# Local attention of a hybrid encoder layer: the strided queries copied side by side by GpSimd ahead of the score products

## The chip, the cores and the metric

The kernel runs on one core of a Trainium2 chip. The metric is the device time of one execution in microseconds (us), as the median over several runs. The core has a matrix engine (TensorE; PE in the profile, with its weight loads shown apart as PEld), VectorE (DVE), ScalarE (ACT), GpSimd (POOL) and SyncE (SP), which here issues most of the DMAs. Each engine works through its own queue in order.

## The reference

One layer on 2048 tokens of width 1024: an input projection feeds two attention parts side by side, whose outputs are normed, projected and added to the residual; a convolutional feed-forward part follows. The change touches part A, local attention over 8 heads of 64 dimensions, which is computed three times with windows of different dilation and mixed by the softmax denominators:

```python
SWA_PATTERNS = ((128, 1), (512, 4), (2048, 16))      # window, dilation

def dilated_band_attention(q, k, v, dilation, n_side):
    ...
    qr = to_residue(q).reshape(B * dilation, nblk, blk, H, Dh).astype(jnp.float32)
    ...
    s = jnp.einsum('znqhd,znkhd->znhqk', qr, kb) * (Dh ** -0.5)
    s = jnp.where(valid[None, :, None, :, :], s, NEG_INF)
```

`to_residue` puts tokens that are `dilation` apart next to each other, so a block of 128 queries of the second pattern is every 4th token, and one of the third every 16th. Part B is a dense attention (multi-head latent attention, "MLA" below) with 4 heads over all 2048 keys.

## The kernel before, in words

**Arithmetic.** Every float32 product is made of products of operands that are split into a rounded part (hi) and the rest (lo). In the local attention the stationary operand of a score product is a block of 128 queries (`qhh`, then `qll`), the moving operand are the keys `kst`.

**Local attention** is `swa` (L519). For a head, `prep` (L540) loads queries and keys in 8 pieces (`raw`, L547, two buffers), transposes them on TensorE and stores `qhh`, `qll` and `kst`, head dimension on partitions and the 2048 tokens along the free axis. Then come 12 groups, four each of pattern 3 (dilation 16), 2 (dilation 4) and 1 (dilation 1), in this order. A group has 4 blocks of 128 queries, and `scores` (L589) issues for each block two matmuls at L601, one with `qhh` and one with `qll` as weights. `operands` (L577) picks the slices:

```python
                return [q[:, P * b:P * b + P] for q in qs], ks[:, 192 + P * b:448 + P * b], side
...
                return [q[:, o:o + 509:4] for q in qs], ks[:, o:o + 1021:4], side
...
            return [q[:, r::16] for q in qs], ks[:, 256 + r:256 + S:16], "all"
```

Pattern 1 reads weights and keys side by side, pattern 2 every 4th column of both, pattern 3 every 16th of both. A block moves 256 keys in patterns 1 and 2 and 128 in pattern 3. VectorE then takes each block out of PSUM with its mask and its maximum (L604). While head h is scored, head h-1 goes on through `numerators` (exponentials), `flip` (transposes, L622), `load_v` and `values` (L635 for pattern 3, L641 for 1 and 2).

**MLA** is `mla_prologue` (L252, which loads and splits its weights, then per 512 tokens transposes `ct`, L286, and writes queries, keys and values to DRAM) and `_mla_core` (L351): score products at L417, transposes at L441, value products at L67 to L69. GpSimd splits the queries `q` of each pair of blocks (L61, L62, L401, L402) and, at a new head, its keys `knh`, `knl` and values `vh`, `vl` (L61, L62).

**Order.** `attention` (L775) is a loop that takes steps of the two parts in a fixed proportion; a scheduler with a model of the engines' times then sets the order in which each engine's queue gets the instructions. Tiles come from pools with a number of buffers (`bufs`); a tile waits until the readers of the one that had its buffer are done. After local attention has ended, the rest of MLA runs with the output projection (`phase_out`) beside it, and the feed-forward part follows.

Of the kernel before, what the change touches and what calls it, by code (L numbers as in the profile page):

```python
# [11 lines left out]
F32 = mybir.dt.float32  # L12
F32R = mybir.dt.float32r
# [7 lines left out]
P = 128  # L21
# [230 lines left out]
def mla_prologue(tc, g, ps_t, ps_s):  # L252


    nc = tc.nc
    with ExitStack() as ctx:
        def pool(name, bufs, **kw):
            return ctx.enter_context(tc.tile_pool(name="mp_" + name, bufs=bufs, reuse_waits="tile", **kw))

        wp = pool("w", 1)  # L260
        op = pool("o", 2)
        raw = wp.tile([P, 2, 768], F32, name="uq_raw")
        nc.sync.dma_start(raw, g.w_uq[0].rearrange("(k p) c -> p k c", p=P))
        uq = (wp.tile([P, 2, 768], F32R, name="uq_hi"), wp.tile([P, 2, 768], F32R, name="uq_lo"))
        nc.scalar.copy(uq[0], raw)
        nc.vector.tensor_tensor(uq[1], raw, uq[0].bitcast(F32), ALU.subtract)
        raw2 = wp.tile([P, 1024], F32, name="ukv_raw")
        nc.sync.dma_start(raw2, g.w_ukv[0])
        ukv = (wp.tile([P, 1024], F32R, name="ukv_hi"), wp.tile([P, 1024], F32R, name="ukv_lo"))
        nc.scalar.copy(ukv[0], raw2)  # L270
        nc.vector.tensor_tensor(ukv[1], raw2, ukv[0].bitcast(F32), ALU.subtract)
        gq = wp.tile([P, 3], F32, name="gq")
        nc.sync.dma_start(gq[:, 0:2], g.q_norm_g[0].rearrange("(k p) -> p k", p=P))
        nc.sync.dma_start(gq[:, 2:3], g.kv_norm_g[0].rearrange("(k p) -> p k", p=P))

        for G in range(4):
            cs = slice(512 * G, 512 * G + 512)
            ct = [op.tile([P, 2, 512], F32, name="ct", bufs=3) for _ in range(2)]
            for i in range(2):
                nc.sync.dma_start(ct[i], g.cd[4 * G + 2 * i:4 * G + 2 * i + 2].rearrange("T p c -> p T c"))  # L280
            cq = [op.tile([P, 2, 512], F32R, name=f"cq{i}", bufs=1) for i in range(2)]
            ckv = [op.tile([P, 512], F32R, name=f"ckv{i}", bufs=1) for i in range(2)]
            for k in (2, 3, 0, 1):
                ps = ps_t.tile([P, 512], F32, name="pst")
                for t in range(4):
                    nc.tensor.transpose(ps[:, P * t:P * t + P], ct[t // 2][:, t % 2, P * k:P * k + P], g.ident)  # L286
                if k < 3:
                    hi, lo = [(cq[i][:, k, :] if k < 2 else ckv[i]) for i in range(2)]
                    nc.scalar.activation(hi, ps, AF.Copy, scale=gq[:, k:k + 1])
                    nc.vector.scalar_tensor_tensor(lo, ps, gq[:, k:k + 1], hi.bitcast(F32), ALU.mult, ALU.subtract)  # L290
                else:
                    kr = op.tile([P, 512], F32, name="kr", bufs=1)
                    nc.scalar.copy(kr, ps)
                    nc.sync.dma_start(g.krd[:, cs], kr)
                yield
            for h in range(MLA_H):
                ps = ps_s.tile([P, 512], F32, name="pss")
                mm3(nc, ps, [u[:, 256 * h:256 * h + P] for u in ukv], ckv, True, True)
                kn = op.tile([P, 512], F32, name="kn")
                nc.scalar.copy(kn, ps)  # L300
                nc.sync.dma_start(g.knd[h, :, cs], kn)
            yield
            vo = op.tile([P, 4, 4, P], F32, name="vo", bufs=1)
            for t in range(4):
                ts_ = slice(P * t, P * t + P)
                ps = ps_s.tile([P, 4, P], F32, name="pss")
                mm3(nc, ps, [c[:, ts_] for c in ckv],
                    [u.rearrange("p (h c) -> p h c", h=4)[:, :, P:256] for u in ukv], True, True)
                nc.vector.tensor_copy(vo[:, :, t, :], ps)
            nc.sync.dma_start(g.vmd[:, :, 512 * G:512 * G + 512].rearrange("h p c -> p h c"),  # L310
                              vo.rearrange("p h t d -> p h (t d)"))
            yield
            qr = []
            for t in range(4):
                T = 4 * G + t
                ps = ps_s.tile([P, 512], F32, name="pss")
                ts_ = slice(P * t, P * t + P)
                for k in range(2):
                    b = [u[:, k, :].rearrange("p (h c) -> p h c", h=4)[:, :, 128:192] for u in uq]
                    mm3(nc, ps[:, :256].rearrange("p (h c) -> p h c", h=4),  # L320
                        [c[:, k, ts_] for c in cq], b, k == 0, k == 1)
                qs = op.tile([P, 4, 64], F32, name="qs")
                nc.scalar.copy(qs.rearrange("p h c -> p (h c)"), ps[:, :256])
                qd = op.tile([P, 4, 2, 64], F32, name=f"qd{t}", bufs=1)
                rope(nc.vector, op, [qd[:, :, 0, :], qd[:, :, 1, :]], qs, g.cos[:, T], g.sin[:, T], 4, 32, "rqp")
                qr.append(qd)
                if t % 2:
                    yield
            for h in range(MLA_H):
                qo = op.tile([P, 2, 2, 256], F32, name="qo")  # L330
                ps = ps_s.tile([P, 512], F32, name="pss")
                for k in range(2):
                    mm3(nc, ps, [u[:, k, 192 * h:192 * h + P] for u in uq], [c[:, k, :] for c in cq], k == 0, k == 1)
                nc.scalar.copy(qo[:, :, 0, :], ps.rearrange("p (b c) -> p b c", b=2))
                ps = ps_t.tile([P, 512], F32, name="pst")
                for t in range(4):
                    nc.tensor.transpose(ps[:, P * t:P * t + P], qr[t][:, h].rearrange("p a c -> p (a c)"), g.ident)
                nc.vector.tensor_copy(qo[:, :, 1, :], ps.rearrange("p (b c) -> p b c", b=2))
                nc.sync.dma_start(g.qd[h, 2 * G:2 * G + 2].rearrange("b p c -> p b c"), qo.rearrange("p b a c -> p b (a c)"))
                yield  # L340
# [10 lines left out]
def _mla_core(tc, g, ctx, ps_s, ps_t, ps_o, scale):  # L351
# [101 lines left out]
                yield  # L453

    def finish(h, blk, parts, po):
        ot = op.tile([P, 256], F32, name="ot", bufs=1)
        nc.scalar.copy(ot, po[:, :256])
        ps = ps_t.tile([P, 512], F32, name="pst")
        for i in range(2):
# [38 lines left out]
def swa_masks(tc, pool):  # L498
# [1 line left out]

    nc = tc.nc
    masks = {}
    for name, n, base in (("mid", 256, -64), ("all", P, 0)):
        m = pool.tile([P, n], F32, name=f"mask_{name}")
        nc.gpsimd.memset(m, 0.0)

        for sign in (1, -1):
            nc.gpsimd.affine_select(m, m, pattern=[[sign, n]], base=64 + sign * base, channel_multiplier=-sign,
                                    compare_op=ALU.is_ge, fill=NEG)
        masks[name] = m  # L510
    for c, name in enumerate(("first", "last")):
        e = pool.tile([P, 256], F32, name=f"mask_{name}")
        nc.gpsimd.tensor_copy(e, masks["mid"])
# [5 lines left out]
def swa(tc, g, ps_t, ps_o):  # L519
# [3 lines left out]
    with ExitStack() as ctx:  # L523
# [5 lines left out]
        two = cp.tile([P, 64], F32, name="two")  # L529
        for i in range(2):  # L530
            nc.gpsimd.tensor_copy(two[64 * i:64 * i + 64], g.ident[64 * i:64 * i + 64, 64 * i:64 * i + 64])
        lp = pool("l", 2)
        sp = pool("s", 1)
        vp = pool("v", 3)
        scp = pool("sc", 1)
        wp = pool("w", 2)
        op = pool("o", 1)
# [2 lines left out]
        def prep(h):  # L540
# [3 lines left out]
                nc.gpsimd.memset(ks[:, a:a + 256].bitcast(F32), 0.0)  # L544
            for j in range(2):
                for c in range(4):
                    raw = lp.tile([P, 4, P], F32, name="raw")  # L547
                    nc.sync.dma_start(raw, g.qkd[j, 512 * c:512 * c + 512, P * h:P * h + P].rearrange("(T p) c -> p T c", p=P))
                    ps = ps_t.tile([P, 512], F32, name="pst")
                    for i in range(4):  # L550
# [12 lines left out]
        def load_v(h, pat, gi):  # L563
# [10 lines left out]
                nc.sync.dma_start(vf[:, :4], vv[:, 4 * gi:4 * gi + 4])  # L574
            return v

        def operands(pat, gi, blk, qs, ks):  # L577
            if pat == 1:
                b = 4 * gi + blk
# [2 lines left out]
            if pat == 2:  # L582
                side = "first" if blk == 0 else "last" if blk == 3 else "mid"
                o = 512 * blk + gi
                return [q[:, o:o + 509:4] for q in qs], ks[:, o:o + 1021:4], side
            r = 4 * gi + blk
            return [q[:, r::16] for q in qs], ks[:, 256 + r:256 + S:16], "all"

        def scores(pat, gi, qs, ks, mx):  # L589

            n = 256 if pat < 3 else P
            per = 512 // n
            sc = scp.tile([P, 4, n], F32, name=f"sc{n}", bufs=8 if pat < 3 else 4)
            for bank in range(4 // per):
                ps = ps_t.tile([P, per, n], F32, name="pst")
                sides = []
# [122 lines left out]
        for h in range(SWA_H + 1):  # L719
# [14 lines left out]
            for n in range(len(groups) + 2):  # L734
                if prev and n < len(groups):
# [5 lines left out]
                    p = psc.pop((pat, gi))  # L741
                    with tc.issue_after(flipped[n - LOOK]) if n >= LOOK else nullcontext():
                        numerators(p, part((None, None, nb3) if n < 2 else nbs, pat, gi), part(den, pat, gi))
                    work.append([pat, gi, p, load_v(h - 1, pat, gi)])
                    yield
                if prev and n >= 2:
                    pat, gi, t, v = work.pop(0)
                    values(pat, gi, *t, v, o)
                    yield
                if 0 <= n - 1 < len(groups):  # L750
                    pat, gi = groups[n - 1]
                    if prev:
# [696 lines left out]
```

## Time and profile before

| what | us |
|---|---|
| median of 3 runs | 3156.75 |
| lowest and highest run | 3154.77, 3157.22 |
| the profiled execution | 3154.04 |
| its span, from the first to the last instruction | 3152.3 |
| TensorE busy in it | 2970.6 (94%) |
| VectorE, ScalarE, GpSimd busy | 2139.3, 1385.6, 1182.3 |

The rows below come from this one profiled execution, and their times count from the start of its span. A row of the timeline gives the start of an instruction, its duration, engine, line and tiles. Durations of matmuls overlap, since they are pipelined, so their pace is read from the distance between starts. Weight loads (PEld) are instructions of their own that run beside the matmul before.

### The profile page before, as it was taken

The numbers are of one execution on the slowest core, as the hardware profiler recorded it, in microseconds if no ns is written. First come the engines' busy times: TensorE is split into PE (matmuls) and PEld (weight loads), VectorE is DVE, ScalarE is ACT, GpSimd is POOL, SyncE is SP. The second block draws the span as 40 slices with busy tenths as digits, with TensorE's granted clock in tenths as the row PEclk, the third lists the DMA queues.
The fourth block names the chain that finished last, engine by engine and source line by source line (L and its number), as shares of the span: only waits on it lengthen the run. The fifth ranks groups of instructions, "written<-read, shape, count | busy, mean of one in ns | idle before, by whom it ended". The sixth has DMA issues, their size and how long they took to land.

```text
span 3152.3 us, 44575 instructions
## 1 busy us (share of the span) xinstructions
PE 2970.6 (94%) x15652; PEld 2532.7 (80%) x15652; DVE 2139.3 (68%) x4747; ACT 1385.6 (44%) x2896; POOL 1182.3 (38%) x1325
## 2 busy tenths in 40 slices
PE   6999989799999999999998999998999997999887
PEld 5888878799999998988887788888888885777665
DVE  7455367677877877776667666666666668666866
ACT  4222236546565465564333444445444444233332
POOL 3211100200200200214334877777777774233433
PEclk9999989999999999999999999998999998999999
DMA  5333365412322322224335233334333336333333
GB/s 210 151 133 124 126 196 174 144 48 70 95 57 68 87 63 66 67 70 129 102 110 162 74 101 100 101 101 130 97 101 101 104 107 228 105 111 109 120 125 102
DMA packets 398636, 352.38 MB, mean 112 GB/s; under 512 B 49804, under 2 KB 335180, under 8 KB 398412
## 3 DMA queue, kind: packets, MB, share of 16 engines
q1 hardware_dynamic: 386028, 308.64, 32.6%
q10 hardware_dynamic: 12384, 40.90, 3.3%
q8 instruction: 123, 2.02, 0.3%
q14 instruction: 101, 0.83, 0.1%
HBM read 225.94 MB, written 123.54 MB: 111 GB/s over the span
## 4 chain that ended last, share of the span: by engine, by line
PE 74%; DVE 5%; DMA 4%; ACT 2%; issue 2%; POOL 2%; SPq 0%; ACTq 0%; POOLq 0%; DVEq 0%
PE pm L1020 26%; PE pss L417 9%; PE pst L869 6%; PE pst L601 5%; PE pb L1307 4%; PE pst L441 3%; PE pa L1307 3%; PE pe L1307 3%; PE pst L622 2%; PE pso L641 2%; PE pso L68 2%; PE pso L67 2%; PE pso L69 2%; DMA a<-yd 1%; PE pst L704 1%
## 5 line engine op out<-in xcount | busy, mean ns | idle before, releaser
L1025 DVE TENSOR_TENSOR h<-pm,h 128x512 f32<-128x512 f32 (+1 forms) x235 | 154.4, 657 | 278.7 <-PE pm L1020 277.4
L1001 POOL TENSOR_TENSOR wl<-s,wh 128x512 fp32r<-128x512 f32 x132 | 171.4, 1299 | 159.9 <-PE pm L1020 137.8
L1000 ACT CAST wh<-raw 128x512 fp32r<-128x512 f32 x172 | 106.2, 617 | 256.9 <-PE pm L1020 256.5
L417 PE MATMUL pss<-knh,q 128*128 128x512 f32 x512 | 207.5, 407 | 9.7 <-POOL q L61 9.6
L418 DVE CUSTOM_DVE_ANT_0 p<-pss,zero 128x512 f32<-128x512 f32 x256 | 172.2, 686 | 51.1 <-PE pss L417 42.6
L445 DVE TENSOR_TENSOR pt_lo<-pst,pt_hi 128x512 fp32r<-128x512 f32 x256 | 172.2, 685 | 16.0 <-ACT pt_hi L444 13.6
L610 ACT ACTIVATE sc<-sc,nb 128x256 f32<-128x256 f32 (+1 forms) x384 | 177.0, 467 | 10.9 <-DVE nb L676 10.9
L61 POOL TENSOR_SCALAR q<-raw 128x256 fp32r<-128x256 f32 x32 | 13.4, 420 | 430.6 <-issue 324.1
L424 ACT ACTIVATE p<-p,nb 128x1024 f32<-128x1024 f32 x128 | 146.1, 1144 | 47.9 <-DVE nb L422 47.2
L191 PE MATMUL pmm<-whi,xhi 128*128 128x512 f32 (+1 forms) x512 | 156.7, 393 | 7.2 <-ACT xhi L181 4.9
L441 PE MATMUL pst<-ident,p 128*128 128x128 f32 x1024 | 157.6, 273 | 5.2 <-DVE rden L466 2.0
L68 PE MATMUL pso<-pt_lo,vh 128*128 128x256 f32 x512 | 158.2, 309 | 0.6 <-DVE pt_lo L445 0.6
L624 ACT CAST th<-pst 128x512 fp32r<-128x512 f32 x160 | 93.4, 590 | 146.0 <-PE pst L622 143.0
L191 PE MATMUL pmm<-whi,xlo 128*128 128x512 f32 (+1 forms) x512 | 155.3, 385 | 1.0 <-DVE xlo L182 1.0
L191 PE MATMUL pmm<-wlo,xhi 128*128 128x512 f32 (+1 forms) x512 | 155.6, 383 | 0.0
L67 PE MATMUL pso<-pt_hi,vh 128*128 128x256 f32 x512 | 152.8, 298 | 3.0 <-ACT pt_hi L444 3.0
L1227 ACT CAST h<-a 128x896 fp32r<-128x896 f32 x86 | 79.3, 939 | 170.2 <-PE pb L1307 113.3
L444 ACT CAST pt_hi<-pst 128x512 fp32r<-128x512 f32 x160 | 92.2, 582 | 126.8 <-PE pst L441 125.9
L601 PE MATMUL pst<-kst,qhh 128*128 128x256 f32 (+1 forms) x384 | 143.7, 382 | 3.0 <-DVE tl L625 2.6
L69 PE MATMUL pso<-pt_hi,vl 128*128 128x256 f32 x512 | 145.0, 283 | 0.0
L1228 POOL TENSOR_TENSOR h<-a,h 128x896 fp32r<-128x896 f32 x35 | 77.6, 2220 | 167.3 <-ACT h L1227 159.8
L601 PE MATMUL pst<-kst,qll 128*128 128x256 f32 (+1 forms) x384 | 137.4, 365 | 0.0
(528 smaller groups left out, 9402.9 us busy)
## 6 DMA issues: line engine op xcount, KB each, us to landing
raw<-in_w_up SPq DMA_DIRECT2D x86, 512.0 KB, 3.8
a<-yd SPq DMA_DIRECT2D x86, 448.0 KB, 3.6
yd<-h SPq DMA_DIRECT2D x91, 256.0 KB, 2.7
v<-vd SPq DMA_DIRECT2D x64, 320.0 KB, 3.2
qkd<-qk ACTq DMA_DIRECT2D x32, 512.0 KB, 2.7
raw<-qkd SPq DMA_DIRECT2D x64, 256.0 KB, 3.4
yd<-yc SPq DMA_DIRECT2D x63, 256.0 KB, 2.4
raw<-in_w_down SPq DMA_DIRECT2D x22, 512.0 KB, 3.5
```

The source lines that it names most:

```text
L67: nc.tensor.matmul(out, a[0], b[0], start=start, stop=False)
L68: nc.tensor.matmul(out, a[0], b[1], start=False, stop=False)
L69: nc.tensor.matmul(out, a[1], b[0], start=False, stop=stop)
L191: nc.tensor.matmul(ps[:, :w], xT[a][:, k, :], b[j][:, k, :], start=(n == 0 and k == 0), stop=(n == 2 and k == 7))
L417: nc.tensor.matmul(ps, a, k, start=n == 0, stop=n == 4)
L418: nc.vector.tensor_tensor_reduce(out=p[c // 2][:, 512 * (c % 2):512 * (c % 2) + 512], in0=ps, in1=zero.to_broadcast([P, 512]), scale=1.0, ...
L441: nc.tensor.transpose(ps[:, o:o + P], parts[i][0][kt // 8][:, P * (kt % 8):P * (kt % 8) + P], g.ident)
L601: nc.tensor.matmul(ps[:, i, :], q[t], k, start=t == 0, stop=t == 1)
L610: nc.scalar.activation(sc[:, blk, :], sc[:, blk, :], AF.Exp, bias=nb[:, blk:blk + 1], scale=scale, accum_out=den[:, blk:blk + 1])
L869: nc.tensor.matmul(ps, a[:, k, :], b[k][:, cs], start=(n == 0 and k == 0), stop=(n == 2 and k == 7))
L1020: nc.tensor.matmul(o, w[n][a][:, k, :], r, start=first and m == 0 and k == 0, stop=m == 2 and k == 3, skip_group_check=not first)
L1307: nc.tensor.matmul(ps, y[i][n][a], g.w_down_ops[p, n][b], start=fresh and m == 0 and i == 0, stop=m == 2 and i == len(ps_) - 1, skip_group ...
```

## The change

Before the score products of a group of pattern 2 or 3, GpSimd copies the group's 4 x 128 queries of `qhh`, and then of `qll`, into tiles of 512 columns side by side, and the matmuls take their weights from there. The keys are read as before. The two tiles come from the pool that the pieces `raw` of `prep` come from, which now has 4 buffers. Room for them is made elsewhere:

- the raw weights of MLA's prologue pass through the three `ct` buffers, in three loads instead of two;
- its key tile `kr` takes a buffer of `kn`, the rope's scratch tiles have one buffer each instead of two, and MLA's `ot` takes a buffer of `raw` of its own pool;
- the tiles `v` of local attention have 2 buffers instead of 3, and their loads are issued later, behind the value products of two groups before;
- the mask "all" is a slice of the mask "mid".

```diff
@@ mla_prologue
-        raw = wp.tile([P, 2, 768], F32, name="uq_raw")
-        nc.sync.dma_start(raw, g.w_uq[0].rearrange("(k p) c -> p k c", p=P))
+        raw = lambda: op.tile([P, 2, 512], F32, name="ct", bufs=3).rearrange("p a b -> p (a b)")
...
+        for src, n, hi, lo in ((g.w_uq[0, 0:P], 768, uq[0][:, 0], uq[1][:, 0]), (g.w_uq[0, P:], 768, uq[0][:, 1], uq[1][:, 1]),
+                               (g.w_ukv[0], 1024, *ukv)):
+            r = raw()[:, :n]
+            nc.sync.dma_start(r, src)
+            nc.scalar.copy(hi, r)
+            nc.vector.tensor_tensor(lo, r, hi.bitcast(F32), ALU.subtract)
...
-                    kr = op.tile([P, 512], F32, name="kr", bufs=1)
+                    kr = op.tile([P, 512], F32, name="kn")
...
-                rope(nc.vector, op, [qd[:, :, 0, :], qd[:, :, 1, :]], qs, g.cos[:, T], g.sin[:, T], 4, 32, "rqp")
+                rope(nc.vector, wp, [qd[:, :, 0, :], qd[:, :, 1, :]], qs, g.cos[:, T], g.sin[:, T], 4, 32, "rqp")
@@ _mla_core, finish
-        ot = op.tile([P, 256], F32, name="ot", bufs=1)
+        ot = rp.tile([P, 512], F32, name="raw")[:, :256]
@@ swa
-        lp = pool("l", 2)
+        lp = pool("l", 4)
...
-        vp = pool("v", 3)
+        vp = pool("v", 2)
...
+        def gather(pat, gi, qs):
+            out = []
+            for q in qs:
+                t = lp.tile([P, 4, P], F32R, name="raw")
+                if pat == 3:
+                    nc.gpsimd.tensor_copy(t, q.bitcast(F32).rearrange("p (i r) -> p r i", r=16)[:, 4 * gi:4 * gi + 4])
+                else:
+                    nc.gpsimd.tensor_copy(t.rearrange("p b i -> p (b i)"), q.bitcast(F32)[:, gi::4])
+                out.append(t)
+            return out
...
-                return [q[:, o:o + 509:4] for q in qs], ks[:, o:o + 1021:4], side
+                return [q[:, blk] for q in qs], ks[:, o:o + 1021:4], side
...
-            return [q[:, r::16] for q in qs], ks[:, 256 + r:256 + S:16], "all"
+            return [q[:, blk] for q in qs], ks[:, 256 + r:256 + S:16], "all"
...
+            if pat > 1:
+                qs = gather(pat, gi, qs)
...
-                    work.append([pat, gi, p, load_v(h - 1, pat, gi)])
+                    work.append([pat, gi, p])
...
+                if prev and n < len(groups):
+                    work[-1].append(load_v(h - 1, *groups[n]))
```

Since the scheduler plans anew, the order changes in many places. SP's queue at the start of attention, before (`ct` are the inputs of MLA's prologue, `raw` the pieces of local attention's queries and keys):

```order
L157 DMA xs<-in_x 128x1024 x12
L263 DMA uq_raw<-in_w_uq 128x2x768
L268 DMA ukv_raw<-in_w_ukv 128x1024
L273 DMA gq<-in_q_norm_g 128x2x1
L274 DMA gq<-in_kv_norm_g 128x1
L280 DMA ct<-cd 128x2x512 x3
L548 DMA raw<-qkd 128x4x128 x2
L574 DMA v<-vd 128x4x128 x3
```

and in the changed kernel:

```order
L157 DMA xs<-in_x 128x1024 x12
L268 DMA ct<-in_w_uq 128x768 x2
L268 DMA ct<-in_w_ukv 128x1024
L272 DMA gq<-in_q_norm_g 128x2x1
L273 DMA gq<-in_kv_norm_g 128x1
L279 DMA ct<-cd 128x2x512 x2
L547 DMA raw<-qkd 128x4x128 x4
L279 DMA ct<-cd 128x2x512
```

The loads of `ct` now stand behind the weights that use the same three buffers, and four pieces `raw` follow them instead of two.

GpSimd's queue where MLA changes from its first to its second head, before (`q` are MLA's queries, `knh` and `knl` its keys; no work of local attention stands between them):

```order
L62 TENSOR_TENSOR q<-raw,q 128x256
L402 TENSOR_TENSOR q<-raw,q 64x256
L61 TENSOR_SCALAR knh_9274<-raw 128x512
L62 TENSOR_TENSOR knl_9275<-raw,knh_9274 128x512
L61 TENSOR_SCALAR knh_9280<-raw 128x512
```

and in the changed kernel:

```order
L62 TENSOR_TENSOR q<-raw,q 128x256
L401 TENSOR_TENSOR q<-raw,q 64x256
L582 CAST raw<-qhh 128x512
L582 CAST raw<-qll 128x512
L582 CAST raw<-qhh 128x512
L582 CAST raw<-qll 128x512
L61 TENSOR_SCALAR knh_9430<-raw 128x512
L62 TENSOR_TENSOR knl_9431<-raw,knh_9430 128x512
L582 CAST raw<-qhh 128x512
L582 CAST raw<-qll 128x512
L61 TENSOR_SCALAR knh_9436<-raw 128x512
```

The copies (L582 for pattern 3, L584 for pattern 2) stand in one queue with the splits of MLA's operands, some of them behind a split of keys.

## Rows read from the trace of the kernel before

**Rows 1.** The page: the span, and busy time of each engine.

```profile
span 3152.3 us, 44575 instructions
PE 2970.6 (94%) x15652; PEld 2532.7 (80%) x15652; DVE 2139.3 (68%) x4747; ACT 1385.6 (44%) x2896; POOL 1182.3 (38%) x1325
```

**Rows 2.** Windows: length, busy PE, PEld, DVE, ACT, POOL, granted clock, DMA share, GB/s.

```profile
393.00:427.00 34.00, 23.39 (x113) 18.07 (x112) 17.87 (x38) 14.55 (x24) 0.56 (x2) 0.80 0.83 264
427.00:600.00 173.00, 149.51 (x888) 134.28 (x888) 124.30 (x434) 84.78 (x226) 13.40 (x20) 0.93 0.56 173
600.00:1340.00 740.00, 730.32 (x4977) 679.45 (x4975) 573.36 (x1723) 423.79 (x1079) 101.44 (x153) 1.00 0.26 69
1340.00:1650.00 310.00, 304.11 (x1816) 264.05 (x1815) 215.18 (x560) 140.83 (x334) 89.53 (x62) 1.00 0.33 104
```

**Rows 3.** Groups by line and form, 420 to 1340 us, the score matmuls: busy, mean ns.

```profile
L601 PE MATMUL pst<-kst,qhh 128*128 128x256 f32 x256 | 92.7, 373 | 3.0 <-DVE tl L625 2.6 <-DVE mx L604 0.4
L601 PE MATMUL pst<-kst,qll 128*128 128x256 f32 x256 | 87.1, 351 | 0.0
L601 PE MATMUL pst<-kst,qhh 128*128 128x128 f32 x128 | 51.0, 398 | 0.0
L601 PE MATMUL pst<-kst,qll 128*128 128x128 f32 x128 | 50.3, 393 | 0.0
```

**Rows 4.** Timeline of PE: a group of pattern 3, then value products of the same shape.

```profile
602.85 0.39 PE L601 MATMUL pst<-kst,qhh 128*128 128x128 f32 x1
...
603.94 0.40 PE L601 MATMUL pst<-kst,qll 128*128 128x128 f32 x1
...
604.89 0.27 PE L635 MATMUL pso<-tl,v 128*128 128x128 f32 x1
...
605.56 0.28 PE L635 MATMUL pso<-tl,v 128*128 128x128 f32 x1
```

**Rows 5.** Timeline of PEld: the weight loads of the second and fourth of these matmuls.

```profile
603.85 0.31 PEld L601 LDWEIGHTS pst<-kst,qll 128*128 128x128 f32 x1
...
605.50 0.19 PEld L635 LDWEIGHTS pso<-tl,v 128*128 128x128 f32 x1
```

**Rows 6.** Timeline of PE: half a group of pattern 2, then half of pattern 1.

```profile
632.02 0.42 PE L601 MATMUL pst<-kst,qll 128*128 128x256 f32 x1
...
632.50 0.41 PE L601 MATMUL pst<-kst,qll 128*128 128x256 f32 x1
...
671.98 0.28 PE L601 MATMUL pst<-kst,qhh 128*128 128x256 f32 x1
...
672.34 0.28 PE L601 MATMUL pst<-kst,qll 128*128 128x256 f32 x1
```

**Rows 7.** Timeline of PEld: the weight loads of the second and fourth of these.

```profile
632.28 0.34 PEld L601 LDWEIGHTS pst<-kst,qll 128*128 128x128 f32 x1
...
672.22 0.19 PEld L601 LDWEIGHTS pst<-kst,qll 128*128 128x128 f32 x1
```

**Rows 8.** Groups of POOL, 427 to 1340 us: busy, mean ns, idle before and releasers.

```profile
L62 POOL TENSOR_TENSOR knl<-raw,knh 128x512 fp32r<-128x512 f32 x12 | 15.5, 1288 | 1.0
...
L61 POOL TENSOR_SCALAR vh<-raw 128x512 fp32r<-128x512 f32 x12 | 7.4, 620 | 77.6 <-PE pso L69 58.1 <-PE pso L68 19.5
L61 POOL TENSOR_SCALAR knh<-raw 128x512 fp32r<-128x512 f32 x12 | 7.4, 620 | 175.3 <-issue 147.9 <-PE pss L417 27.4
```

**Rows 9.** Waits of PE, 393 to 600 us: total, times, longest.

```profile
PE pst L551 <- DMA raw<-qkd: 8.0, 7, 2.0
...
PE pst L286 <- DMA ct<-cd: 3.2, 2, 2.7
```

**Rows 10.** Groups of DVE at L118: durations min, median, max in ns.

```profile
L118 DVE TENSOR_TENSOR rq_a<-qk,cos x64: 249/270/2482, 61.9 to 389.6; 128x64 f32<-128x64 f32 x64
L118 DVE TENSOR_TENSOR rqp_a<-qs,cos x32: 269/285/293, 422.2 to 552.7; 128x128 f32<-128x128 f32 x32
```

More of the change, by code (lines that the diff above doesn't have):

```diff
@@ L261, in mla_prologue @@
         op = pool("o", 2)
-        raw = wp.tile([P, 2, 768], F32, name="uq_raw")
-        nc.sync.dma_start(raw, g.w_uq[0].rearrange("(k p) c -> p k c", p=P))
+        raw = lambda: op.tile([P, 2, 512], F32, name="ct", bufs=3).rearrange("p a b -> p (a b)")
         uq = (wp.tile([P, 2, 768], F32R, name="uq_hi"), wp.tile([P, 2, 768], F32R, name="uq_lo"))
[L265 to L268, printed above, removed]
         ukv = (wp.tile([P, 1024], F32R, name="ukv_hi"), wp.tile([P, 1024], F32R, name="ukv_lo"))
-        nc.scalar.copy(ukv[0], raw2)
-        nc.vector.tensor_tensor(ukv[1], raw2, ukv[0].bitcast(F32), ALU.subtract)
+        for src, n, hi, lo in ((g.w_uq[0, 0:P], 768, uq[0][:, 0], uq[1][:, 0]), (g.w_uq[0, P:], 768, uq[0][:, 1], uq[1][:, 1]),
[4 more added lines that the diff above has]
+            nc.vector.tensor_tensor(lo, r, hi.bitcast(F32), ALU.subtract)
         gq = wp.tile([P, 3], F32, name="gq")
@@ L502, in swa_masks @@
     masks = {}
[L503 to L510, printed above, removed]
+    m = pool.tile([P, 256], F32, name="mask_mid")
+    nc.gpsimd.memset(m, 0.0)
+    for sign in (1, -1):
+        nc.gpsimd.affine_select(m, m, pattern=[[sign, 256]], base=64 - sign * 64, channel_multiplier=-sign,
+                                compare_op=ALU.is_ge, fill=NEG)
+    masks["mid"] = m
+    masks["all"] = m[:, 64:192]
     for c, name in enumerate(("first", "last")):
@@ L546, in prep @@
                 for c in range(4):
-                    raw = lp.tile([P, 4, P], F32, name="raw")
+                    raw = lp.tile([P, 4, P], F32R, name="raw").bitcast(F32)
                     nc.sync.dma_start(raw, g.qkd[j, 512 * c:512 * c + 512, P * h:P * h + P].rearrange("(T p) c -> p T c", p=P))
```

## The prediction

> **What bounds the kernel now.** I read the page first, then windows by stage, then the waits and the timeline of the stage that the change touches. The page says that TensorE is busy 94% of a span of 3152.3 us [rows 1], an average over unlike stages. The windows tell them apart [rows 2]. From 393 to 600 us local attention and MLA start up: TensorE is busy 23.4 of 34.0 us and 149.5 of 173.0 us, its granted clock is 0.80 and 0.93, and DMA is at 0.83 and 0.56. From 600 to 1340 us, where most heads of local attention are scored, TensorE is busy 730.3 of 740.0 us at a granted clock of 1.00, while VectorE has 573 and GpSimd 101 us of work. So in these 740 us the length of TensorE's own instructions sets the time, and every nanosecond taken off a matmul there counts. After 1340 us no score product of local attention is left.
>
> The changed matmuls are those of L601: 256 with 128 columns (pattern 3), and 512 with 256 columns, half of them of pattern 2 and half of pattern 1 [rows 3]. Their mean durations overlap, so I take the pace, the distance from start to start. In a group of pattern 3 five steps take 603.94 - 602.85 = 1.09 us, 218 ns each; value products of the same shape whose operands all lie side by side take 605.56 - 604.89 = 0.67 us for six, 112 ns each [rows 4]. Pattern 2 needs 0.48 us for two steps, 240 ns; pattern 1, with as many columns side by side, 0.36 us for three, 120 ns [rows 6]. Both strided patterns run at half the pace of their neighbours.
>
> Two reads are strided, the weights and the moving keys, and the change cures only the first. The weight loads show which counts: 0.31 us strided against 0.19 us side by side [rows 5], and 0.34 against 0.19 us [rows 7]. The strided load is 0.12 us longer, and 0.12 more than the 112 ns pace is about the pace seen. What the keys cost shows in the stretch from the end of a weight load to the end of its matmul. Pattern 3: 603.94 + 0.40 - 603.85 - 0.31 = 0.18 us, beside 605.56 + 0.28 - 605.50 - 0.19 = 0.15 us [rows 4, 5]. Pattern 2: 632.50 + 0.41 - 632.28 - 0.34 = 0.29 us, beside 672.34 + 0.28 - 672.22 - 0.19 = 0.21 us for pattern 1 [rows 6, 7]. So strided keys cost 0.03 us for 128 columns and 0.08 us for 256. Pattern 3 waits for its weights; pattern 2 is nearly held by its keys alone.
>
> **The change, part by part.** *Pattern 3, weights side by side.* The pace lies between 112 ns (neighbour) and 142 ns (neighbour plus 0.03 us that nothing hides). I take 120 ns, near the neighbour, since a 0.19 us load leaves time under the matmul. Gain: 256 x (218 - 120) = 25.1 us.
>
> *Pattern 2.* The pace lies between 120 ns (pattern 1, if keys don't matter) and 240 ns (if they hold it already). The rows give 120 + 80 = 200 ns; I take 210, because its loads run 0.34 us where those of pattern 3 run 0.31, so the two reads already disturb each other. Gain: 256 x (240 - 210) = 7.7 us. The bounds are 0 and 30.7 us. [...]
>
> *The copies.* GpSimd gets 8 groups x 2 x 8 heads = 128 copies of 128x512. No row shows a strided copy. The nearest are a cast of this shape side by side, 620 ns, and a two-input operation, 1288 ns [rows 8]; I take 950 ns, between them, and no smaller end since nothing makes a strided read faster than a plain one. That is 122 us on an engine that has 115 us of work in the 913 us from 427 to 1340 us [rows 2]: it fits, off the path, as long as a pair is done before TensorE comes to its group. Four buffers hold two groups, so the copies of a group start when the group two before has been scored. The 768 matmuls of 8 heads [rows 3] lie in the 913 us, so a head takes 114 us and each of its 12 groups about 10 us, while a pair takes 1.9 us: hidden. Only in the first head, with no older head to fill the gaps, do I charge the path: the first pair, 1.9 us, and about 1 us behind it, together 3 us.
>
> *More buffers for `raw`, and the start.* TensorE waits 8.0 us for these loads between 393 and 600 us [rows 9]; with four in flight I expect half to go, 4 us. Against that, the `ct` loads of MLA's prologue now stand behind the splits of the weights in the same buffers, and `raw` behind them in SP's queue. TensorE's wait for `ct`, 3.2 us [rows 9], can grow by one landing, some 4 us. I set the two against each other: 0, with 6 us either way for the planned order of a stage that is not dense.
>
> *The end.* The planned order lets local attention finish earlier relative to MLA, so a change of MLA's head happens with nothing to fill it. Its keys then need 4 x (0.62 + 1.29) = 7.6 us of GpSimd [rows 8], of which value products cover part: I charge 4 us, bounds 0 and 7.6.
>
> *Costed at nothing:* two buffers for `v` instead of three (a group's 10 us covers the load); `kr`, `ot`, the rope's scratch and the mask, whose users are not what TensorE waits for in these windows.
>
> The sum for the profiled execution: 3154.0 - 25.1 - 7.7 + 3 + 0 + 4 = 3128.2 us. The median of the runs shown is 2.7 us above that execution, so **3131 us**. By the bounds above the forecast's own range is 3118 to 3146 us.
>
> **The rivals.** *A late copy takes the place of a slow load (slower).* GpSimd's queue is in order, and the copies stand in it with splits of MLA's keys and values, which sat 77.6 us (values) and 27.4 us (keys) until TensorE was done with the old ones [rows 8]. A copy behind such a split comes late, and TensorE, in order too, stops at its group. All 64 pairs exposed would cost 64 x 1.24 to 2.58 us; the gain of 25.8 us net is gone at 0.40 us per group. Half of them exposed at 1.9 us gives 61 us, so 3192 us. For it: a whole head's copies are in the queue with the splits. Against it: GpSimd was idle 86% of these 740 us, and a group is 10 us long. Chance 0.08.
>
> *GpSimd and VectorE get in each other's way (about no change).* In the input stage a VectorE operation on two SBUF tiles that takes 270 ns took up to 2482 ns; the same sort in the prologue, where GpSimd had next to nothing to do, stayed under 293 ns [rows 10]. The prologue's rope has 128 such operations on VectorE; if a third meet a copy and wait 0.5 us, 21 us are added to VectorE between 427 and 600 us, where it has 49 us free [rows 2]. If most of it came through, 3148 us. [...] Chance 0.08.
>
> *The change doesn't do what it says.* If the keys, not the weights, held pattern 3, nothing would be gained and the 7 us of costs are left, 3164 us, or about 3160 if the start is as much better as I allow it to be. Against it speak the 0.03 us, which are a few rows only. Chance 0.06.
>
> *More.* If keys are free once the weights are side by side, pattern 2 falls to 120 ns, 23 us more: 3108 us. Chance 0.12.
>
> **How the numbers follow.** The forecast has the remaining 0.66. A measurement of this kernel can tell about 0.2%, 6.3 us, from no change, so "faster" is below 3150.4. Faster: 0.66 + 0.12 + half of the collision, 0.82. Same: the other half, 0.04, and most of "doesn't do what it says", 0.04, so 0.08. Slower: 0.08 + 0.02 = 0.10. The range goes from 3106 us, which takes in the rival with more gain, to 3150 us, which takes in the collision; it leaves out the late copies, the case of no gain, and the edges, some 0.17.
>
> **What would show it.** In the changed profile the weight loads of patterns 2 and 3 should take 0.19 us, pattern 3 pace at 112 to 142 ns, pattern 2 at 200 to 240 ns, and the window that holds the local attention should be about 30 us shorter with TensorE as dense as before. GpSimd should show 128 copies of 0.62 to 1.29 us. The prediction is wrong if TensorE waits on GpSimd for more than some 10 us in total, if the pace of pattern 3 stays near 218 ns, or if the start between 393 and 600 us grows by more than 10 us.

## The result, and the profile after

The changed kernel takes 3198.35 us (median of 4 runs, 3194.06 to 3202.15) against 3156.98 us before (4 runs beside them): a ratio of 1.0127 with a 95% interval of 1.0108 to 1.0147, some 41 us slower. 3131 us and "faster" were predicted. All rows that follow come from profiled executions; that of the changed kernel took 3197.18 us. Times of kernels are medians.

The windows of [rows 2], in the changed kernel (columns as there):

```profile
393.00:427.00 34.00, 22.26 (x117) 18.37 (x116) 17.17 (x37) 13.03 (x22) 8.81 (x10) 0.80 0.73 236
427.00:600.00 173.00, 149.64 (x885) 128.09 (x884) 128.39 (x431) 89.21 (x244) 48.99 (x52) 0.89 0.54 170
600.00:1340.00 740.00, 715.49 (x4948) 653.09 (x4948) 571.47 (x1689) 437.36 (x1154) 176.34 (x219) 0.99 0.27 72
1340.00:1650.00 310.00, 277.40 (x1589) 237.30 (x1587) 189.30 (x515) 110.51 (x212) 97.43 (x80) 0.95 0.27 86
```

TensorE is idle 24.5 us of the dense stretch where it was idle 9.7, and 32.6 us of the last window where it was idle 5.9. It shows fewer matmuls in both windows. The score products did get cheaper. The groups of the changed matmuls, from 420 to 1340 us (they answer to [rows 3]), with the copies:

```profile
L614 PEld LDWEIGHTS pst<-kst,raw 128*128 128x128 f32 x512 | 81.9, 203 | 10.4 <-issue 3.5 <-DVE mx L617 0.8 <-POOL q L61 0.7
L614 PE MATMUL pst<-kst,raw 128*128 128x256 f32 x256 | 71.5, 416 | 2.2 <-DVE tl L638 1.7 <-DVE mx L617 0.4
L584 POOL CAST raw<-qll 128x512 fp32r<-128x512 f32 x32 | 36.3, 1134 | 0.0
L584 POOL CAST raw<-qhh 128x512 fp32r<-128x512 f32 x32 | 36.1, 1128 | 111.3 <-PE pst L614 111.1
L614 PE MATMUL pst<-kst,raw 128*128 128x128 f32 x256 | 38.9, 309 | 0.9 <-DVE kst L558 0.7
```

Pattern 3 fell from 398 and 393 ns to 309. The weight loads of the two patterns fell from 0.31 and 0.34 us [rows 5, 7] to a mean of 0.20. The matmuls of pattern 2 did not get shorter: a mean of 0.416 us, beside 0.42 and 0.41 us in [rows 6]. The timeline of PE, a whole group of pattern 3 and half a group of pattern 2 (they answer to [rows 4, 6]):

```profile
711.69 1.09 PE L614 MATMUL pst<-kst,raw 128*128 128x128 f32 x8
...
736.10 1.09 PE L614 MATMUL pst<-kst,raw 128*128 128x256 f32 x4
```

Eight matmuls of pattern 3 now take the 1.09 us that five steps took. Over all 256 of each kind, the median distance from start to start went from 217 to 112 ns in pattern 3, and from 236 to 233 ns in pattern 2.

**Where the time went.** To count it, I gave each matmul of a line its usual distance (the median of that line before, of the pattern itself for score products) and called the rest of a stretch lost: TensorE idle, waiting a little, or at a lower granted clock (in the changed kernel 0.50 from 1380 to 1405 us, for one). A row of this count is good to about 2 us, which is what another grouping of the matmuls changes. From 393 us to the first matmul of the feed-forward part (at 1716.5 us before, 1761.8 after; from there on both kernels need the same time within 3 us):

| us | before | after |
|---|---|---|
| work of TensorE | 1235.3 | 1210.5 |
| lost, 393 to 620 | 49.5 | 59.3 |
| lost, 620 to 1340 | 23.7 | 52.6 |
| lost, from 1340 on | 15.0 | 46.4 |

The work fell by 24.8 us, where the forecast had 32.8 us for both patterns; what is missing is mostly pattern 2. The losses grew by 70 us. The largest single one is this stop of TensorE: first PE's rows, then ACT's, then POOL's queue in those microseconds.

```profile
1399.97 0.69 PE L459 MATMUL pst<-ident,raw 128*128 128x128 f32 x2 [24.97 <-ACT raw L456]
```

```profile
1399.55 0.37 ACT L456 COPY raw<-pso 128x256 f32<-128x256 f32 x1 [26.18 <-POOL knl L62]
```

```profile
1374.96 2.35 POOL L62 TENSOR_TENSOR wl<-x,wh 128x1024 fp32r<-128x1024 f32 x1
...
1391.26 0.62 POOL L61 TENSOR_SCALAR knh<-raw 128x512 fp32r<-128x512 f32 x1
1391.84 2.35 POOL L62 TENSOR_TENSOR wl<-x,wh 128x1024 fp32r<-128x1024 f32 x1
1394.15 0.62 POOL L61 TENSOR_SCALAR knh<-raw 128x512 fp32r<-128x512 f32 x1
1394.73 2.34 POOL L62 TENSOR_TENSOR wl<-o,wh 128x1024 fp32r<-128x1024 f32 x1
1397.03 2.49 POOL L62 TENSOR_TENSOR knl<-raw,knh 128x512 fp32r<-128x512 f32 x2
```

The tile `raw` that ScalarE writes at L456 is MLA's `ot`: the change put it into the two `raw` buffers. It waits for a key piece of the last MLA head in that buffer, whose split stands in POOL's queue among the splits of the output projection's weights. Those are there so early because local attention's last score comes at 1269.0 us instead of 1337.8, while MLA's last head starts at 1401 us instead of 1302. MLA has fallen behind long before that stop: its second, third and last head start at 856, 1122 and 1401 us instead of 807, 1054 and 1302. How it fell behind shows in its q. Here are the load on SP, the split on POOL and the first use on PE for one pair of blocks of the third head. Before:

```profile
1095.96 0.40 SPq L399 DMA_DIRECT2D raw<-qd  x1
```

```profile
1134.95 0.40 POOL L61 TENSOR_SCALAR q<-raw 128x256 fp32r<-128x256 f32 x1 [24.43 <-issue]
```

```profile
1173.20 0.39 PE L417 MATMUL pss<-knh,q 128*128 128x512 f32 x1
```

and after, for the pair that comes just before that one in the third head:

```profile
1196.93 0.46 SPq L398 DMA_DIRECT2D raw<-qd  x1
```

```profile
1200.60 0.41 POOL L61 TENSOR_SCALAR q<-raw 128x256 fp32r<-128x256 f32 x1 [0.61 <-DMA raw<-qd]
```

```profile
1205.80 0.43 PE L416 MATMUL pss<-knh,q 128*128 128x512 f32 x1
```

Over the 32 loads the median lead of load over use is 73 us before and 6.6 us after. The theories of what loses the time are: **A**, the shared `raw` buffers of `ot`; **B**, the gathers on POOL; **C**, the two late `v` buffers.

### The profile page after: what moved, and what is told of

Read it like the earlier page. It is cut to its first block, busy times and chain, and to the rows that moved or that the text cites. A ratio compares the mean times of both kernels' runs of the same rounds, so it can differ in the third digit from the quotient of the medians.

```text
span 3195.4 us, 44843 instructions
## 1 busy us (share of the span) xinstructions
PE 2973.5 (93%) x15652; PEld 2512.3 (79%) x15652; DVE 2140.3 (67%) x4748; ACT 1387.3 (43%) x2899; POOL 1316.5 (41%) x1450
## 4 chain that ended last, share of the span: by engine, by line
PE 49%; DVE 4%; DMA 3%; POOL 2%; ACT 2%; issue 1%; SPq 0%; POOLq 0%; ACTq 0%; DVEq 0%
PE pm L1035 26%; PE pst L884 5%; PE pb L1322 4%; PE pss L416 3%; PE pe L1322 3%; PE pa L1322 2%; DMA a<-yd 1%; PE pst L440 1%; PE pso L68 1%; DVE z L1333 1%; PE pso L69 1%; PE pso L67 1%; DVE h L1243 1%; ACT h L1242 1%; POOL h L1243 1%
## 5 line engine op out<-in xcount | busy, mean ns | idle before, releaser
L444 DVE TENSOR_TENSOR pt_lo<-pst,pt_hi 128x512 fp32r<-128x512 f32 x256 | 173.5, 686 | 29.7 <-ACT pt_hi L443 26.9
L1015 ACT CAST wh<-s 128x512 fp32r<-128x512 f32 x132 | 81.3, 618 | 128.8 <-PE pm L1035 127.8
L1084 DVE SCALAR_TENSOR_TENSOR pc<-h,cw,pc 128x1024 f32<-128x1024 f32 x88 | 113.2, 1287 | 35.0 <-ACT pc L1083 35.0
L440 PEld LDWEIGHTS pst<-ident,p 128*128 128x128 f32 x1024 | 122.1, 142 | 13.2 <-DVE ob L466 1.3
```

Of the source, the lines that this page charges most:

```text
L440: nc.tensor.transpose(ps[:, o:o + P], parts[i][0][kt // 8][:, P * (kt % 8):P * (kt % 8) + P], g.ident)
L444: nc.vector.tensor_tensor(lo, ps, hi.bitcast(F32), ALU.subtract)
L1015: nc.scalar.copy(hi, srcs[n])
```

## The experiments

**e1: `ot` out of `raw`, all else as changed.**

```
-        ot = rp.tile([P, 512], F32, name="raw")[:, :256]
+        ot = op.tile([P, 2, P], F32, name="ob", bufs=1).rearrange("p a c -> p (a c)")
```

> The changed kernel, with MLA's `ot` taken out of the two `raw` buffers: it shares the one buffer of `ob` instead, which costs no room. Theory A (the shared `raw` buffers lose the time): the stop of 25.0 us at the change to the last MLA head, the 3.9 us of the other waits for `ot`, and part of the half-clock stretch behind it go, and the 20 us that the score products gained stay: 3150 to 3170 us, and the local attention's scores end later than at 1269 us. Rival B (the gathers on POOL's queue, and the order of work that comes with them, lose the time): the stop only changes its name, to a wait for a key piece behind the splits of the output projection's weights: 3190 to 3200 us. Rival C (two `v` buffers filled late): 3185 to 3200 us.

3144.18 us (10 runs), ratio 0.9969 (0.9957 to 0.9981): 54 us faster than the change (52 us when each is taken against the runs of before beside it), and faster than before. That is better than theory A's range, which ended at 3150 us. The q lead is 69 us again. Waits of POOL for q from 600 to 1600 us, changed kernel and then e1 (total, times, longest):

```profile
POOL q L61 <- DMA raw<-qd: 209.5, 17, 37.3
```

```profile
POOL q L61 <- DMA raw<-qd: 13.2, 6, 6.1
```

With the buffer apart, from 600 to 1340 us TensorE is as dense as before, with 132 matmuls more than in [rows 2]:

```profile
600.00:1340.00 740.00, 730.32 (x5109) 669.83 (x5109) 590.70 (x1755) 444.47 (x1158) 193.97 (x237) 1.00 0.27 74
```

**e2: the trims without gathers.**

```
-            if pat > 1:
-                qs = gather(pat, gi, qs)
...
-                return [q[:, blk] for q in qs], ks[:, o:o + 1021:4], side
+                return [q[:, o:o + 509:4] for q in qs], ks[:, o:o + 1021:4], side
...
-            return [q[:, blk] for q in qs], ks[:, 256 + r:256 + S:16], "all"
+            return [q[:, r::16] for q in qs], ks[:, 256 + r:256 + S:16], "all"
```

> The changed kernel without the gathers: all the trims of buffers, the four `raw` buffers, and the queries strided as in the kernel before. Theory A and rival C (a trim loses the time): the loss stands without the gain, 3157 + 41 + some 20 = 3205 to 3225 us. Rival B (the gathers lose it): 3150 to 3165 us.

3206.4 us, ratio 1.0165 (1.015 to 1.018). The loss is there without one gather, so B falls. The stop is not there: TensorE waits for `ot` 1.6 us at most.

**e3: the kernel before, with `ot` shared and nothing else.**

```
-        ot = op.tile([P, 256], F32, name="ot", bufs=1)
+        ot = rp.tile([P, 512], F32, name="raw")[:, :256]
```

> The kernel before with one edit: MLA's `ot` in the two `raw` buffers. Theory A: q loads that come late for the shared buffer, MLA falls behind the local attention and the last head's pieces queue behind the output projection's weights: 3180 to 3210 us. Rivals B and C: 3153 to 3161 us, no change.

3206.84 us, ratio 1.0166 (1.0151 to 1.0181). One line makes the whole loss, some 52 us. Here too there is no long stop: TensorE's longest wait for `ot` is 1.0 us. POOL's wait for q from 600 to 1600 us, and the windows:

```profile
POOL q L61 <- DMA raw<-qd: 379.2, 18, 35.6
```

```profile
600.00:1340.00 740.00, 718.66 (x4846) 661.52 (x4847) 558.38 (x1681) 415.73 (x1086) 84.42 (x132) 1.00 0.25 67
1340.00:1650.00 310.00, 284.64 (x1659) 245.38 (x1658) 199.46 (x516) 135.80 (x291) 98.57 (x80) 0.96 0.29 94
```

**e4: the kernel before, with two late `v` buffers.**

```
-        vp = pool("v", 3)
+        vp = pool("v", 2)
...
-                    work.append([pat, gi, p, load_v(h - 1, pat, gi)])
+                    work.append([pat, gi, p])
...
+                if prev and n < len(groups):
+                    work[-1].append(load_v(h - 1, *groups[n]))
```

> The kernel before with one edit: two buffers of `v` instead of three, each load issued after the values step that frees one. Rival C: values products that wait for `v`, 3175 to 3200 us. Theory A and rival B: 3153 to 3163 us, since the v load (3.3 us) has a whole group, some 10 us, to land.

3159.0 us, ratio 1.0018 (1.0008 to 1.0028): 4 to 6 us dearer, not nothing, and far from the 41 us. C falls as the cause.

**e5: e1 with gathers of pattern 3 alone** (and pattern 2's operands as in e2).

```
-            if pat > 1:
+            if pat == 3:
```

> e1 (`ot` apart) with the gathers of pattern 3 alone; pattern 2 reads its queries strided, as before. If the copies hide on POOL: pattern 2's pace goes back from 233 to 236 ns, 3 us dearer, and the whole stays at 3143 to 3149 us. Rival (64 copies of 1.13 us on POOL hold up q's splits and the key pieces): 3130 to 3141 us.

3143.01 us, ratio 0.9963 (0.995 to 0.9976), not to be told from e1: pattern 2's 64 copies show neither gain nor harm.

**e6: e3 with three `raw` buffers** (the room comes from the mask and two small tiles).

```
-    rp = pool("r", 2)
+    rp = pool("r", 3)
```

> e3 (the kernel before with `ot` in `raw`) with three `raw` buffers instead of two; the room comes from the mask `all`, as in the change, and from second buffers of two small tiles (`m12`, `d23`). Theory A as a shortage of buffers: the fourth user finds a buffer, 3152 to 3165 us. Rival D (what loses is the place of `ot` in the rotation, behind key pieces and q loads, however many buffers there are): 3185 to 3207 us.

3181.59 us, ratio 1.0088 (1.0076 to 1.01): between both expectations. A third buffer gives half of the loss back, but not q's lead, which stays at 6.7 us, and the last head starts at 1361 us, only 6 us earlier than in e3. So scarcity is a part, and the place of the q load another. Most of what comes back lies behind 1340 us, where TensorE is idle 10.1 us instead of 25.4 in e3:

```profile
600.00:1340.00 740.00, 722.39 (x4871) 667.22 (x4870) 561.91 (x1686) 418.73 (x1097) 84.24 (x132) 0.99 0.25 67
1340.00:1650.00 310.00, 299.90 (x1751) 259.09 (x1749) 209.42 (x546) 139.33 (x296) 101.64 (x82) 0.98 0.31 98
```

**e10: the changed kernel, q requested earlier from the same buffers.**

```
                 parts.append(scores(q, i, kn))
                 yield
+                if i == 0 and pr < 7:
+                    ahead = load_q(h, pr + 1)
```

> The changed kernel with the same buffers; only q of the next pair is asked for (buffer, load, split) behind the first block's scores of this pair, ahead of this pair's `ot`. In the trace of e1 a q load goes out 69 us before its use (median), in those of the changed kernel, e3 and e6 6.6 to 6.7 us. Theory E (the place of the q load behind `ot` in the order of requests for `raw` is what holds MLA back): the load goes out some 30 us ahead of use, MLA's last head starts 50 us or more earlier than at 1401 us, 3150 to 3175 us. Rival F (it is the time for which `ot` holds a buffer, or the key and value pieces behind it): 3185 to 3200 us.

3169.87 us, ratio 1.0053 (1.0039 to 1.0067): 28 us of the 54 come back by the order of requests alone (24 of 52 against the runs of before beside each). The lead is 22.5 us and the last head starts at 1370 us, 31 us earlier, less than expected. Here more comes back from 600 to 1340 us, where TensorE is idle 12.3 us instead of 24.5, than behind, where it is idle 23.8 us instead of 32.6:

```profile
600.00:1340.00 740.00, 727.73 (x5068) 665.26 (x5067) 584.19 (x1730) 447.40 (x1169) 178.29 (x220) 0.99 0.27 72
1340.00:1650.00 310.00, 286.20 (x1627) 245.17 (x1627) 194.50 (x532) 119.56 (x225) 102.32 (x82) 0.96 0.29 94
```

The two largest waits left stand at the change to the last head. There q can't be asked for early by this edit, and its splits queue on POOL among those of the output projection's weights (waits of PE, 600 to 1600 us):

```profile
PE pss L416 <- POOL q L61: 13.4, 2, 13.0
PE pss L416 <- POOL q L62: 6.8, 1, 6.8
```

The traces show what a q load hangs on. From the third pair of a head on, the request for q stands in the program right behind that of the `ot` of two pairs back; e10 moves it ahead of this one, behind the `ot` of three pairs back. In the changed kernel, e2, e3, e6 and e9 the load goes out 3 to 4 us (median) ahead of ScalarE's write of that `ot`; before and in e1, where `ot` lies elsewhere, some 90 us ahead; in e10 33 us ahead of it, and 2 us ahead of the `ot` that now comes before it. So the load comes out at the place of the request before it in the pool, with two buffers and with three.

**e9: the changed kernel, the output projection's splits off POOL.**

```
-        split(nc.gpsimd, w[0][k], w[1][k], raw)
+        nc.scalar.copy(w[0][k], raw)
+        nc.vector.tensor_tensor(w[1][k], raw, w[0][k].bitcast(F32), ALU.subtract)
```

> The changed kernel as it is, with one edit: the eight splits of the output projection's weights on ScalarE and VectorE instead of POOL, so that the last MLA head's key pieces don't queue behind them. If the queue behind those splits is what the shared buffer costs: the stop of 25.0 us and the slow clock behind it go, 3160 to 3175 us. Theory A as a lag (MLA is already 99 us late at its last head, since q loads wait for `ot`, and its tail then runs alone): most of the loss stays, 3180 to 3198 us.

3187.54 us, ratio 1.0105 (1.0092 to 1.0118). The stop of 25.0 us is gone (the longest wait for `ot` is 2.4 us), but only 11 us of time come back (8 us against the runs of before beside each): the stop was a place where the lag was paid, not its cause. e2 and e3, which lose as much without such a stop, say the same.

**e7: e1 with the first `ct` loads ahead of the weights.** The loads of the first pair move ahead of the loop over the weights, and `w_ukv` ahead of `w_uq`.

```
+        first = load_ct(0)
...
+            ct = load_ct(G) if G else first
```

> e1 with the first two `ct` loads issued ahead of the three weight loads that share their buffers, and `w_ukv` ahead of `w_uq`. If the wait of 7.3 us at 393 us for `ct` behind the weights is on the path: 3135 to 3141 us. Rival (the next wait, for the weights or for the local attention's loads, takes its place): 3142 to 3148 us.

3145.65 us, ratio 0.9974 (0.9964 to 0.9984), as e1. The wait for `ct` went, and another took its place: the loads of local attention, for which PE waits 2.3 us in e1 from 393 to 600 us, now cost in the same window

```profile
PE pst L555 <- DMA raw<-qkd: 8.4, 5, 3.0
```

**e8: e5 with three early `v` buffers and three `raw` buffers of local attention.**

```
-        lp = pool("l", 4)
+        lp = pool("l", 3)
-        vp = pool("v", 2)
+        vp = pool("v", 3)
```

> e5 (`ot` apart, gathers of pattern 3 alone) with three `v` buffers filled as early as in the kernel before, and three `raw` buffers of the local attention instead of four for the room. If the two late `v` buffers cost what e4 showed (4 us): 3136 to 3141 us. Rival (the third `raw` pair's half is missed by the gathers, or v's 4 us were hidden here): 3142 to 3150 us.

3151.14 us, ratio 0.9995 (0.9986 to 1.0003): a miss of both expectations, 8 us slower than e5. The `v` buffers, the `raw` buffers and two small tiles were changed at once, so it tells only that the exchange doesn't pay.

**e11: e1 with the keys side by side too**, and three `raw` buffers of local attention instead of four for the room.

```
+            kg = lp.tile([P, 640], F32R, name="kg", bufs=1)
...
+                nc.gpsimd.tensor_copy(kg, ks.bitcast(F32)[:, gi::4])
```

> e1 with each group's keys copied side by side too (one more copy on POOL per strided group, of 640 or 512 columns), three `raw` buffers instead of four. Theory G (after the gathers of the queries it is the strided keys that set the pace, about 0.9 ns a column against 0.46 in pattern 1): pattern 2 falls from 233 to 120 to 135 ns, 25 to 29 us, pattern 3 from 112 to 60 to 80 ns, 8 to 13 us, and the whole to 3105 to 3120 us. Rival (the weight loads of 192 to 207 ns, or something else, hold the pace, or the third copy comes late): 3138 to 3150 us.

3141.41 us, ratio 0.9964 (0.9952 to 0.9977): the rows agree with the theory for pattern 2, the time doesn't. Groups of the score products (420 to 1380 us) and the new copy:

```profile
L591 POOL CAST kg<-kst 128x640 fp32r<-128x640 f32 x32 | 43.6, 1364 | 0.1
L618 PE MATMUL pst<-kg,raw 128*128 128x256 f32 x256 | 41.8, 302 | 0.0
```

Pattern 2's distance falls from 233 to 119 ns: its keys held it. Pattern 3 stays at 112 ns where 60 to 80 were expected, so putting its keys side by side gains nothing. 29 us of work go, but the lost time grows by 5 us up to 620 and by 18 us from 620 to 1340 us. The median is 3 us below that of e1, which the intervals don't tell from nothing. The keys were not the only edit: e8, with the same three `raw` buffers and the same small tiles, was slower than e5, so the missing buffer may take part of the gain. No run tests this.

**e12, e13, e14: VectorE relieved** in e11, in the kernel before and in e1.

```
-            (nc.vector.tensor_copy if c in (0, 2, 6) else nc.scalar.copy)(hi, ps)
+            (nc.vector.tensor_copy if c == 2 else nc.scalar.copy)(hi, ps)
```

> e11 with two of the three `pt_hi` copies of MLA's values that stand on VectorE (0.68 us each, 64 of 96) moved to ScalarE: 44 us less on VectorE. If VectorE (80% busy between 600 and 1340 us) takes the place of the score products, so that their 28 us in the rows give 3 us in the time: 3122 to 3136 us. Rival H (the gain is lost at the start and in the tail, where MLA or the output projection runs alone, not to VectorE): 3138 to 3146 us.

> The kernel before with the same edit of two `pt_hi` copies as e12, to tell its own effect. If VectorE is second to PE only where the score products are cheap: 3150 to 3160 us, no change. If VectorE held PE up here too: 3135 to 3148 us.

> e1 (`ot` apart, both gathers) with the same edit as e12. If VectorE takes back part of the 21 us that the gathers gain in the rows of e1, of which 11 us are in its time: 3128 to 3139 us. Rival H: 3141 to 3148 us.

3157.12, 3166.01 and 3153.14 us; ratios 1.0003 (0.9992 to 1.0013), 1.0038 (1.0026 to 1.005) and 0.9995 (0.9986 to 1.0004). All three are slower than without the edit, by 9 to 16 us, and outside both of their expectations. Moving this load from VectorE to ScalarE gives nothing back. A ScalarE that comes later with these copies may be as bad as a busy VectorE, so these runs don't settle whether VectorE's load takes the gain.

**e15, e16: e1 with the gathers from the third, or the second, head on**.

```
-            if pat > 1:
+            if pat > 1 and near:
...
-                        scs[pat, gi] = scores(pat, gi, qs, ks, part(mx, pat, gi))
+                        scs[pat, gi] = scores(pat, gi, qs, ks, part(mx, pat, gi), h >= 2)
```

> e1 with the gathers from the third head of the local attention on; the first two heads read their queries strided, as before. Counted by rows, PE loses 63 us of the 227 us from 393 to 620 us in e1, 44 in e2 (same buffers, no gathers) and 50 in the kernel before. If the gathers cost that stretch more than the cheaper products give there: the lost time of the stretch falls to 45 to 55 us and the whole to 3130 to 3139 us. Rival (the stretch is held by loads and by the projections' own chain, and dearer products there only take the place of idle time): 3141 to 3149 us.

> e1 with the gathers from the second head on. If it is the first head alone, whose gathers follow right behind the preparation of the queries, that costs the start: like e15 or better, 3128 to 3138 us. If the second head, behind the change to the MLA core, is part of it: between e1 and e15. Rival as for e15: 3141 to 3149 us.

3143.64 and 3141.83 us; ratios 0.9966 (0.9954 to 0.9979) and 0.9958 (0.9946 to 0.9971). Up to 620 us the lost time is 56.5 and 57.5 us, 6 us below e1, yet the whole doesn't differ from e1's: the rival's range holds, and the first heads' gathers show neither cost nor gain. e16 has the lowest ratio of all; its interval overlaps those of e1, e5, e11 and e15.

## Why the prediction was wrong

The step that failed is **"Costed at nothing: ... `ot`, ... whose users are not what TensorE waits for in these windows"**. It looked at who waits for `ot` before, not at who shares the buffer afterwards: q, keys and values of MLA go through it, and q's loads ran 73 us ahead as long as only loads stood in that pool. e3 prices the line at 52 us, and e1 shows it from the other side at 54 us. e10 shows that 24 to 28 of them hang on q's place in the order, e6 that a third buffer gives back half.

Point by point:

- *What bounds the kernel*: right for 600 to 1340 us, as long as loads run ahead. "Every nanosecond counts" held only in part. e1 saves 25.7 us of work against before and its median is 11 us below. In its profiled execution (7 us above its median) it loses 13.6 us more up to 620 us and 6.6 us more behind 1340 us, and no more in between. What takes these back is not shown.
- *Pattern 3*: right. 112 ns where 120 were taken, within the bounds of 112 and 142; 26.9 us by medians instead of 25.1.
- *Pattern 2*: mis-sized. 233 ns instead of 210; the gain is 0.8 us by medians instead of 7.7. The stretch from load to end (0.08 us) did not give the cost of the keys; with both sides cured the distance is 119 ns, so the keys cost 114 ns a matmul. With the queries side by side and the keys strided, pattern 2 gained next to nothing (from 236 to 233 ns).
- *The copies*: right in that they hide, a little dearer: 1.07 to 1.13 us instead of 0.95. Of the idle time ahead of L614 from 420 to 1340 us (releaser, us, times) this is what pattern 2's gathers have, and pattern 3's have no row:

```profile
  POOL raw L584: 0.5, 1
```

- *The start*: 0 with 6 either way was too narrow. 9.8 us more were lost up to 620 us. The wait for `ct` grew as forecast, by some 4 us ([rows 9] has 3.2):

```profile
PE pst L285 <- DMA ct<-cd: 7.6, 2, 7.4
```

  but e7 shows that it is not what the stretch hangs on. What does is open.
- *The end*: the right place and half the mechanism. 4 us (bounds 0 and 7.6) were charged for key pieces at a head change with nothing to fill it. The stop there was 25.0 us, because the output projection's splits stood between the pieces and `ot` behind them; e9 prices that queue at 8 to 11 us.
- *Two `v` buffers at nothing*: 4 to 6 us in e4, a small miss.
- *The range*: added up, the prediction's own bounds reach 3154 us on the slow side, not 3146. The measured time lies 44 us beyond that, so it is not a matter of sizes within the bounds.
- *The rivals*: "slower" did come, by none of them. Late copies: no, as the row above shows. GpSimd against VectorE: the rope's operations of [rows 10] kept their median (286 ns), with a longest of 1001 ns instead of 293. A change that does nothing: no, pattern 3 took its 112 ns. Of the signs given for "wrong", the lost time up to 620 us did grow by almost 10 us, and TensorE's waits for GpSimd, almost all for q, came to 9.5 us by PE's rows from 393 to 1762 us. The longest wait was for ScalarE, behind GpSimd, and no sign named a late load.

Open are why the planner puts a q load at the place of the request before it (the traces show where it goes out, not why), how the rest of the loss comes about that e10 doesn't give back, what takes e11's 29 us back, and where the first 227 us lose what they lose.

## What to carry to other kernels

Before costing a buffer's new tenant at nothing, list the pool's other tenants and how far ahead of use their loads run; here a step that comes late in the program, put among loads that ran ahead, pulled them back to its own place, with three buffers as with two (a lead of 73 us became 6.7 and 6.6). When a stop is found, look for the lag behind it: moving the queue it stands in gave back 8 to 11 us, moving the tenant 52 to 54. Work taken off the busiest engine need not come back in full: of 25.7 us the median of e1 gives 11, and 29 us more in e11 gave nothing clear of noise.

## What was not expected of the hardware

Once the weights lie side by side, strided moving keys cost nothing in pattern 3 (stride 16, 128 columns: 112 ns strided and side by side) and half the speed in pattern 2 (stride 4, 256 columns: 233 against 119 ns). One pace for strided columns would fit both: 233 ns for 256 columns is 0.91 ns each, which gives 117 ns for 128, an estimate, close to the 112 ns that pattern 3 takes either way. Side by side, 128 columns take 112 ns and 256 only 119, so at 128 columns it is not the columns that set the pace. What does is not shown.

TensorE stood still from 1375 us until 1399.97 us. The granted clock was 0.50 from 1380 to 1405 us, 0.86 from 1405 to 1410, and 1.00 from 1410 to 1415 (some of the windows of the changed kernel, columns as in [rows 2]):

```profile
1380.00:1385.00 5.00, 0.00 (x0) 0.00 (x0) 0.00 (x0) 0.00 (x0) 5.00 (x6) 0.50 0.58 163
...
1400.00:1405.00 5.00, 4.22 (x10) 3.10 (x11) 0.61 (x2) 0.00 (x0) 3.02 (x6) 0.50 0.50 132
1405.00:1410.00 5.00, 5.00 (x20) 3.66 (x19) 3.20 (x11) 0.13 (x1) 3.24 (x4) 0.86 0.37 93
1410.00:1415.00 5.00, 3.80 (x18) 2.80 (x17) 4.02 (x11) 2.25 (x4) 4.25 (x6) 1.00 0.37 95
```
